# Products in turn, later joins and a third pair of seven products in a two-layer encoder kernel

## The chip, the core and the metric

The kernel runs as one program on one core of a Trainium2 chip. The metric is the device time of one execution in microseconds (us). TensorE does the matrix products, VectorE (DVE in the profile) and ScalarE (ACT) do the elementwise work, SyncE (SP) issues nearly all transfers, and GpSimd (POOL) does a few small operations.

## The reference: what is computed

Two layers run over a sequence of 256 tokens with a model width of 2048, all in float32. In each layer:

- `h = RMSNorm(x)`, then one input projection gives queries, keys, values and two gating inputs (width 3584 in all);
- eight heads of windowed attention, with two key/value heads, rotary embedding, norms of queries and keys, and a learned sink in the softmax;
- a spatial gating part: GELU, a LayerNorm, a 128x128 product per head along the sequence, and a multiplication;
- both results are normalised, joined and projected back by `w_o`, and the residual is added;
- a feed-forward part: `x + W_down(silu(g) * u)`, where `[g | u]` is a three-tap depthwise convolution over the sequence of `RMSNorm(x) @ w_up`, with a hidden width of 5632.

## The kernel before, in words

**Three products for one.** The products must be as good as float32, and TensorE takes them in a shorter type. So every operand is split into a high part and a low part. For activations and weights `(a_hi + a_lo)(w_hi + w_lo)` the kernel computes `a_hi w_hi`, `a_lo w_hi` (these two are called high products here, since they use the high part of the weights) and `a_hi w_lo` (the low product). Each weight piece is loaded into a `raw` tile, ScalarE copies it to `hi` (line 154), and VectorE subtracts to get `lo` (line 142). There are four `raw` buffers, three `hi` and three `lo`.

**Blocks.** The usual block is 1 MB of weights: four slices of 128 rows by 512 columns. `rows_by_cols` (line 175; its matmul is line 181) runs 24 matmuls on it: 16 high products over all four slices, then the 8 low products. The input projection, `w_o` and `w_up` use it; `direct` (its matmul is line 209) does the same for `w_down`. In the input projection and the first half of `w_o` a block is split in two pieces of 1024 columns (`step`), and the first two blocks of the program in four. `unit` (lines 325 and 330) handles the gate input the other way round, with the weights stationary: 32 high products of 512 columns, then 32 low products of 256.

**Seven products.** In the down projection some pairs of slices for a pair of column groups are done by a scheme with seven products in place of eight (`seven`, lines 239 to 287). It needs sums of weight slices (lines 249 to 251), splits two tiles (lines 245 and 252 on ScalarE, two subtractions of line 142 on VectorE), so it takes two `hi` and two `lo` buffers, and runs 21 matmuls (lines 269, 270 and 275) where 24 would stand. The mixes of the activations that it needs are made by `mixed` when these activations are finished. `seven_out` adds its four sums into the residual.

**The feed-forward part** runs in two halves of the hidden width (`HALVES`): 20 slices, then 24. In each half, `gate_and_up` makes four slices at a time: g rows and u rows by 4 blocks each, then `leave` takes them out of PSUM (lines 914 and 916 on ScalarE) and asks for transposes by DMA; when these have landed, ScalarE puts the words together (`together`, line 495), and the convolution, the activation and the multiplication follow on both engines. Then the down projection of that half runs in two groups, each for a pair of column groups. `FAST` says which pairs of slices go by seven: two pairs in both groups of the first half, four pairs in the first group of the second half.

**The order of the work.** Steps that are to follow later are put in a list, `waiting`; `let_in` runs everything in it, and is called inside each block after its second slice. `after(n, step)` makes a step wait for n more such calls. The queue of each engine is put in order at build time by the framework's scheduler: of the instructions that it takes to be ready it chooses the one with the highest priority, with its own estimates for when things are ready. Priority follows the program's order, with the parts under `urgent()` first. `issue_after` ties only instructions of TensorE to their place. On the chip, each queue runs strictly in the order that the scheduler made.

Of the kernel before, what the change touches and what calls it, by code (L numbers as in the profile page):

```python
# [25 lines left out]
NK = D // P  # L26
NF = DFF // P
W = 512
KB = 4
# [4 lines left out]


HALVES = ((0, 20), (20, NF))
FAST = ((4, 10), (4, 8, 12, 16))
AFTER = (2, 4, 5, 6)


# [26 lines left out]
def encoder(ctx: ExitStack, tc: tile.TileContext, xT, x, w_in, w_gu, w_o, w_up, w_down, wsT, pcol, prow, rope, out):  # L67
# [97 lines left out]
    def after(n, step):  # L165
        waiting.append(step if n == 0 else lambda: after(n - 1, step))

    def let_in():
        for step in waiting[:]:
            waiting.remove(step)  # L170
            with tc.issue_after(latest()), urgent():
                step()


    def rows_by_cols(ps, acts, src, first, last, raw=None, apart=False, step=4 * W):

        hi, lo = split_weights(src, raw, step)

        def product(m, kk, part):
            w = (hi if part < 2 else lo)[:, kk * W : (kk + 1) * W]  # L180
            nc.tensor.matmul(  # L181
                ps[m], acts[kk][:, part % 2, m * P : (m + 1) * P], w,
                start=first and kk == 0 and part == 0, stop=last and kk == KB - 1 and part == 2,
            )

        if apart:
            for m in range(2):
                for kk in range(KB):
                    for part in range(3):
                        product(m, kk, part)  # L190
            return
        for kk in range(KB):
            for m in range(2):
                product(m, kk, 0)
                product(m, kk, 1)
            if kk == 1:
                let_in()
        for kk in range(KB):
            for m in range(2):
                product(m, kk, 2)  # L200
# [38 lines left out]
    def seven(left, right, more, acts, mix, src, used_left, used_right, first, last):  # L239
        with urgent():  # L240
            raw = raw_tile()
            nc.sync.dma_start(raw, src)
            sums = raw_tile()
            hi, lo, his, los = hi_tile(), lo_tile(), hi_tile(), lo_tile()
            nc.scalar.activation(hi[:, : 3 * W], raw[:, : 3 * W], AF.Copy)
            b = raw.rearrange("p (g c) -> p g c", c=W)
            s = sums.rearrange("p (g c) -> p g c", c=W)
            b12 = b[:, 3:4, :].to_broadcast([P, 2, W])
            nc.vector.tensor_tensor(out=s[:, 0:2, :], in0=b12, in1=b[:, 0:3:2, :], op=ALU.add)
            nc.vector.tensor_tensor(out=s[:, 2, :], in0=s[:, 0, :], in1=b[:, 2, :], op=ALU.add)  # L250
            nc.vector.tensor_tensor(out=s[:, 3, :], in0=s[:, 2, :], in1=b[:, 1, :], op=ALU.add)
            nc.scalar.activation(his, sums, AF.Copy)  # L252
            lo_part(lo[:, : 3 * W], raw[:, : 3 * W], hi[:, : 3 * W])
            lo_part(los, sums, his)

        def own(kk, m):
            return [acts[kk][:, j, m * P : (m + 1) * P] for j in range(2)]

        def mix_of(j):
            return [t[:, j * P : (j + 1) * P] for t in mix]  # L260

        used_more = set() if first else set(range(4))
        low = []

        def product(ps, used, m, a, w, g):
            cs = slice(g * W, (g + 1) * W)
            new = m not in used
            used.add(m)
            nc.tensor.matmul(ps[m], a[0], w[0][:, cs], start=new, stop=False)  # L269
            nc.tensor.matmul(ps[m], a[1], w[0][:, cs], start=False, stop=False)  # L270
            low.append((ps, m, a, w, cs))

        def lows():
            for ps, m, a, w, cs in low:
                nc.tensor.matmul(ps[m], a[0], w[1][:, cs], start=False, stop=ps is more and last)  # L275
            low.clear()

        product(left, used_left, 0, own(1, 0), (hi, lo), 1)
        product(right, used_right, 0, mix_of(3), (hi, lo), 2)
        product(more, used_more, 0, own(0, 0), (hi, lo), 0)  # L280
        lows()
        product(more, used_more, 1, mix_of(2), (his, los), 2)
        product(more, used_more, 2, mix_of(1), (his, los), 0)
        product(more, used_more, 3, mix_of(0), (his, los), 1)
        product(left, used_left, 1, own(1, 1), (his, los), 3)
        lows()
# [17 lines left out]
    def take(steps):  # L304
        for step in steps:
            with tc.issue_after(latest()):
                step()


    def unit(acts, w, steps=()):  # L310
        ps = mm()
        his, los = [], []
        for b in range(0, NK, UB):
            h, lo = split_weights(w[:, b * UW : (b + UB) * UW], None, 2 * W)
            his.append(h)
            los.append(lo)

        def tile_of(tiles, k, i):
            c = k % UB * UW + i * P
            return tiles[k // UB][:, c : c + P]  # L320

        for k in range(NK):
            for i in range(2):
                x1 = acts[k].rearrange("p a b -> p (a b)")
                nc.tensor.matmul(ps[:, i, :], tile_of(his, k, i), x1, start=k == 0, stop=False)  # L325
            if k == 5:
                let_in()
        for k in range(NK):
            for i in range(2):
                nc.tensor.matmul(  # L330
                    ps[:, i, :SEQ], tile_of(los, k, i), acts[k][:, 0, :], start=False, stop=k == NK - 1
                )
            if k == 0:
                take(steps)
        return ps


# [344 lines left out]
    NB = NK // KB  # L682
    for l in range(DEPTH):
        pc, qk = params
        acts = hT

        def in_rows(ps, c, b):
            src = w_in[l, c, :, b * KB * W : (b + 1) * KB * W]
            raw = first_raws.pop(0) if l == 0 and first_raws else None
            step = 2 * W if raw is None else W  # L690
            rows_by_cols(ps, acts[b * KB : b * KB + KB], src, b == 0, b == NB - 1, raw, step=step)


        psk, psq = mm(), mm()
# [27 lines left out]
        atts = []  # L722
# [41 lines left out]
        first = group_steps(0, psq)  # L764
        first()
        ps = chunk(1, [[sent_keys], [turned_keys, first], [], [first]] if l else [[], [], [sent_keys, first], [turned_keys]])
# [8 lines left out]
        for i in range(2):  # L775
# [4 lines left out]
            ps = chunk(3 + i, between[i])  # L780
# [73 lines left out]
        gates = []  # L854
# [6 lines left out]
        def out_rows(half, c, r):  # L861
            t = mm()
            ps = [t[:, m, :] for m in range(2)]
            for b in range(2):
                src = w_o[l, c, :, (half * 2 + b) * KB * W : (half * 2 + b + 1) * KB * W]
                rows_by_cols(ps, (atts, gates)[half][b * KB : b * KB + KB], src, b == 0, b == 1, step=4 * W if half else 2 * W)
            residual(ps, c, r)

        ra = inv_rms_cols(acca, D // 2, "a")
# [36 lines left out]
            src = w_up[l, n * (NF // 4) + j, :, b * KB * W : (b + 1) * KB * W]  # L906
            rows_by_cols([ps[:, m, :] for m in range(2)], acts2[b * KB : b * KB + KB], src, b == 0, b == NB - 1)

        def leave(ps, then):
            halves = []  # L910
            for m in range(2):
                rows = ev().rearrange("p a b -> p (a b)")
                with urgent():
                    nc.scalar.activation(rows, ps[:, m, :], AF.Copy, scale=r2[:, m : m + 1])  # L914
                h = sl([P, 2, 2, SEQ], U16)
                nc.scalar.copy(h, rows.bitcast(U16).rearrange("p (j n b) -> p j b n", j=2, b=2))  # L916
                halves.append(h)
            tall = [sl([P, 4, SEQ], U16) for _ in range(2)]

            def asked():  # L920
                for j in range(2):
                    for m in range(2):
                        half = halves[m][:, j, :, :].rearrange("p b n -> p (b n)")
                        nc.sync.dma_start_transpose(tall[j][:, :, m * P : (m + 1) * P], half)
                after(2, lambda: then(tall))

            waiting.append(asked)

        def gate_and_up(j, ys, mixes):
# [22 lines left out]
            if j == 0:  # L952
                pss = [mm(), mm()]
                for b in range(NB):
                    for n in range(2):
                        up_rows(pss[n], n, j, b)
                        if b == NB - 1:
                            leave(pss[n], (gate_in, up_in)[n])
                return
            for n in range(2):  # L960
                ps = mm()
                for b in range(NB):
                    up_rows(ps, n, j, b)
                leave(ps, (gate_in, up_in)[n])

        w_at = 0
        for half, (f0, f1) in enumerate(HALVES):
# [5 lines left out]
            last = f1 == NF  # L973
# [19 lines left out]
            for group in range(2):  # L993
# [4 lines left out]
                for n, (cs, ks, sevenfold) in enumerate(blocks):  # L998
# [6 lines left out]
                    src = w_down[l, :, w_at : w_at + len(cs) * len(ks) * W]  # L1005
                    w_at += len(cs) * len(ks) * W
                    acts = [ys[k - f0] for k in ks]
# [88 lines left out]
```

## Time and profile before

| | |
|---|---|
| Median of 3 runs | 1971.12 us (1969.78 to 1973.15) |
| Time of the profiled execution | 1969.81 us |
| Its span, first to last instruction | 1968.0 us |
| TensorE busy with matmuls | 1954.8 us, 8832 matmuls |
| VectorE busy | 1334.6 us |
| ScalarE busy | 1318.1 us |
| Data moved | 414.02 MB, 210 GB/s on average |
| Granted TensorE clock | 1.000 |

The time of an execution is 1.8 us longer than its span; the span runs from the first to the last instruction. Matmuls overlap in the records: one of 512 columns is recorded with 389 ns, but the next one starts earlier, so the distance between starts is what counts. In a group of instructions the last columns are busy time, mean duration of one, and idle time of the engine just before these instructions with what ended it. In the waits, each line gives the total, the number of times, and the longest.

### The profile page before, as it was taken

To read this page: it belongs to the slowest core of one execution; us is meant where nothing else is said; L and a number is where in the kernel's file an instruction comes from. 1 tells how busy PE (TensorE), PEld (TensorE's weight loads), DVE (VectorE), ACT (ScalarE), POOL (GpSimd) and SP (SyncE) were. 2 spreads that over 40 slices of the span, in tenths; PEclk is the share of its full clock that TensorE was granted. 3 is DMA by queue.
4 is the path that set the end of the run, shared out by engine and by line. 5 is a ranking of instruction groups with operands and counts; after the bars stand their busy time and mean duration, and the time that the engine had idled before them with its cause. 6 is when DMAs were issued, how large, how long until landed. Compare 5 with 4: busy or idle time off the path is not lost.

```text
span 1968.0 us, 22935 instructions
## 1 busy us (share of the span) xinstructions
PE 1954.8 (99%) x8832; PEld 1622.1 (82%) x8832; DVE 1334.6 (68%) x1628; ACT 1318.1 (67%) x1437; POOL 22.9 (1%) x25
## 2 busy tenths in 40 slices
PE   9999999999999999999999999999999999999999
PEld 7878888888788888888888888888888888888887
DVE  6768775666874666688566696756668655666873
ACT  6667487687644777776666774877885456777742
POOL 0000000000000000000000000000000000000000
PEclk9999999999999999999999999999999999999999
DMA  9763486776665677757767546867766667677572
GB/s 373 218 213 141 171 235 190 220 227 195 217 235 187 217 226 223 213 174 246 231 205 221 172 150 203 242 199 222 217 197 218 214 205 223 214 217 224 169 267 86
DMA packets 190733, 414.02 MB, mean 210 GB/s; under 512 B 139424, under 2 KB 140704, under 8 KB 145568
## 3 DMA queue, kind: packets, MB, share of 16 engines
q1 hardware_dynamic: 189904, 411.83, 66.1%
q8 instruction: 69, 1.13, 0.2%
q10 hardware_dynamic: 720, 0.73, 0.1%
q14 instruction: 40, 0.33, 0.1%
HBM read 378.43 MB, written 2.10 MB: 193 GB/s over the span
## 4 chain that ended last, share of the span: by engine, by line
PE 87%; ACT 5%; DMA 3%; DVE 3%; issue 2%; SPq 0%; DVEq 0%; ACTq 0%
PE mm L181 59%; PE mm L209 17%; DMA sl<-sl 3%; PE mm L325 3%; ACT hi L154 2%; PE tp L209 2%; DVE lo L142 2%; PE mm L330 1%; ACT sl L916 1%; PE mm L275 1%; PE mm L270 1%; PE mm L269 1%; ACT sl L914 1%; ACT sl L495 1%; DVE sl L897 0%
## 5 line engine op out<-in xcount | busy, mean ns | idle before, releaser
L142 DVE TENSOR_TENSOR lo<-raw,hi 128x2048 fp32r<-128x2048 f32 (+3 forms) x444 | 839.0, 1904 | 491.0 <-ACT hi L154 442.2
L181 PE MATMUL mm<-hi,sl 128*128 128x512 f32 x3968 | 943.4, 389 | 0.9 <-ACT hi L154 0.8
L154 ACT ACTIVATE hi<-raw 128x2048 fp32r<-128x2048 f32 (+2 forms) x412 | 650.3, 1594 | 364.8 <-PE mm L181 171.7
L181 PEld LDWEIGHTS mm<-hi,sl 128*128 128x128 f32 x3968 | 744.4, 188 | 156.1 <-ACT hi L154 1.7
L181 PE MATMUL mm<-lo,sl 128*128 128x512 f32 x1984 | 491.3, 389 | 0.0
L181 PEld LDWEIGHTS mm<-lo,sl 128*128 128x128 f32 x1984 | 372.1, 188 | 76.9
L209 PE MATMUL mm<-hi,sl 128*128 128x512 f32 x1056 | 250.4, 389 | 1.9 <-ACT hi L154 1.9
L209 PEld LDWEIGHTS mm<-hi,sl 128*128 128x128 f32 x1056 | 198.1, 188 | 43.8 <-ACT hi L154 2.8
L495 ACT COPY sl<-sl 128x1024 uint16<-128x1024 uint16 x98 | 132.5, 1352 | 134.7 <-DMA sl<-sl 134.5
L209 PE MATMUL mm<-lo,sl 128*128 128x512 f32 x528 | 130.4, 389 | 0.0
L209 PEld LDWEIGHTS mm<-lo,sl 128*128 128x128 f32 x528 | 99.1, 188 | 20.5
L896 ACT ACTIVATE sl<-sl,pc 128x256 f32<-128x256 f32 x176 | 95.8, 590 | 1.3
L916 ACT COPY sl<-sl 128x1024 uint16<-128x1024 uint16 x88 | 92.0, 1046 | 2.6
L897 DVE SCALAR_TENSOR_TENSOR sl<-sl,pc 128x255 f32<-128x255 f32 x176 | 77.9, 478 | 8.1 <-ACT sl L896 8.0
L900 DVE SCALAR_TENSOR_TENSOR sl<-sl,pc 128x255 f32<-128x255 f32 x176 | 77.9, 478 | 0.7
L325 PE MATMUL mm<-sl,hi 128*128 128x512 f32 x256 | 63.7, 394 | 1.6 <-ACT sl L784 1.6
L356 ACT ACTIVATE sl<-sl 128x256 fp32r<-128x256 f32 x88 | 31.7, 408 | 46.7 <-DVE sl L944 46.7
L914 ACT ACTIVATE sl<-mm,yr 128x512 f32<-128x512 f32 x88 | 59.7, 678 | 0.0
L325 PEld LDWEIGHTS mm<-sl,hi 128*128 128x128 f32 x256 | 46.8, 188 | 10.6 <-ACT sl L784 1.8
L349 DVE SCALAR_TENSOR_TENSOR sl<-sl,pc 128x256 fp32r<-128x256 f32 x96 | 42.1, 479 | 17.6 <-ACT sl L348 17.4
L348 ACT ACTIVATE sl<-sl,pc 128x256 fp32r<-128x256 f32 x96 | 43.0, 498 | 2.3 <-DMA sl<-in_xT 1.1
L252 ACT ACTIVATE hi<-raw 128x2048 fp32r<-128x2048 f32 x16 | 30.6, 1914 | 19.2 <-PE mm L209 14.1
(144 smaller groups left out, 1062.5 us busy)
## 6 DMA issues: line engine op xcount, KB each, us to landing
raw<-in_w_up SPq DMA_DIRECT2D x176, 1024.0 KB, 5.0
raw<-in_w_down SPq DMA_DIRECT2D x88, 1024.0 KB, 4.8
raw<-in_w_in SPq DMA_DIRECT2D x38, 1024.0 KB, 5.1
raw<-in_w_o SPq DMA_DIRECT2D x32, 1024.0 KB, 5.0
raw<-in_w_gu SPq DMA_DIRECT2D x16, 1024.0 KB, 5.4
sl<-sl SPq DMA_TRANSPOSE x244, 4.3
sl<-in_prow SPq DMA_DIRECT2D x12, 256.0 KB, 7.4
raw<-in_w_in SPq DMA_DIRECT2D x8, 256.0 KB, 5.3
```

What stands on the lines that cost most here:

```text
L142: nc.vector.tensor_tensor(out=lo, in0=part, in1=hi.bitcast(F32), op=ALU.subtract)
L154: nc.scalar.activation(hi[:, cs], raw[:, cs], AF.Copy)
L181: nc.tensor.matmul(ps[m], acts[kk][:, part % 2, m * P : (m + 1) * P], w, start=first and kk == 0 and part == 0, stop=last and kk == KB - 1 ...
L209: nc.tensor.matmul(ps[m], acts[kk][:, part % 2, m * P : (m + 1) * P], w, start=first, stop=done and kk == len(acts) - 1 and part == 2,)
L325: nc.tensor.matmul(ps[:, i, :], tile_of(his, k, i), x1, start=k == 0, stop=False)
L348: nc.scalar.activation(t[:, 0, :], src, AF.Copy, scale=g)
L495: nc.scalar.copy(words, tall.rearrange("p (b a) n -> p b (a n)", b=2))
L896: nc.scalar.activation(t[:, i, :], s[:, i, :], AF.Identity, bias=col(3), scale=col(1))
L897: nc.vector.scalar_tensor_tensor(out=t[:, i, 1:], in0=s[:, i, : SEQ - 1], scalar=col(0), in1=t[:, i, 1:], op0=ALU.mult, op1=ALU.add)
L900: nc.vector.scalar_tensor_tensor(out=t[:, i, : SEQ - 1], in0=s[:, i, 1:], scalar=col(2), in1=t[:, i, : SEQ - 1], op0=ALU.mult, op1=ALU.add)
L914: nc.scalar.activation(rows, ps[:, m, :], AF.Copy, scale=r2[:, m : m + 1])
L916: nc.scalar.copy(h, rows.bitcast(U16).rearrange("p (j n b) -> p j b n", j=2, b=2))
```

## The change

There are five edits.

1. `FAST` for the first half becomes (4, 8, 12) in place of (4, 10): three pairs of slices by seven products instead of two. The four column pairs concerned are two in each of the two layers. The 14 slices that are left are no multiple of 4, so the last plain block of each column group has two slices.
2. `rows_by_cols` gets `in_turn`: for each slice the four high products are followed at once by its two low products. The input projection (all blocks through `in_rows`) and the first half of `w_o` use it. The unused branch `apart` of this function goes.
3. `seven` calls `let_in` once, after its first low products.
4. `unit` runs its low products with the column half outside and the slice inside, and takes the `steps` after the second low product of the first half.
5. `leave` gets the number of calls to wait before the transposes are put together: 3 for the last group of four slices in each half, 2 as before for the others. The first group (`j == 0`) keeps 2.

```diff
-FAST = ((4, 10), (4, 8, 12, 16))
+FAST = ((4, 8, 12), (4, 8, 12, 16))
...
-    def rows_by_cols(ps, acts, src, first, last, raw=None, apart=False, step=4 * W):
+    def rows_by_cols(ps, acts, src, first, last, raw=None, in_turn=False, step=4 * W):
...
-        if apart:
-            for m in range(2):
-                for kk in range(KB):
-                    for part in range(3):
-                        product(m, kk, part)
-            return
         for kk in range(KB):
             for m in range(2):
                 product(m, kk, 0)
                 product(m, kk, 1)
+            if in_turn:
+                for m in range(2):
+                    product(m, kk, 2)
             if kk == 1:
                 let_in()
+        if in_turn:
+            return
         for kk in range(KB):
             for m in range(2):
                 product(m, kk, 2)
...
         product(more, used_more, 0, own(0, 0), (hi, lo), 0)
         lows()
+        let_in()
         product(more, used_more, 1, mix_of(2), (his, los), 2)
...
-        for k in range(NK):
-            for i in range(2):
+        for i in range(2):
+            for k in range(NK):
                 nc.tensor.matmul(
                     ps[:, i, :SEQ], tile_of(los, k, i), acts[k][:, 0, :], start=False, stop=k == NK - 1
                 )
-            if k == 0:
-                take(steps)
+                if i == 0 and k == 1:
+                    take(steps)
...
-            rows_by_cols(ps, acts[b * KB : b * KB + KB], src, b == 0, b == NB - 1, raw, step=step)
+            rows_by_cols(ps, acts[b * KB : b * KB + KB], src, b == 0, b == NB - 1, raw, True, step)
...
-                rows_by_cols(ps, (atts, gates)[half][b * KB : b * KB + KB], src, b == 0, b == 1, step=4 * W if half else 2 * W)
+                rows_by_cols(ps, (atts, gates)[half][b * KB : b * KB + KB], src, b == 0, b == 1, None, half == 0, 4 * W if half else 2 * W)
...
-        def leave(ps, then):
+        def leave(ps, then, wait):
...
-                after(2, lambda: then(tall))
+                after(wait, lambda: then(tall))
...
-                            leave(pss[n], (gate_in, up_in)[n])
+                            leave(pss[n], (gate_in, up_in)[n], 2)
...
-                leave(ps, (gate_in, up_in)[n])
+                leave(ps, (gate_in, up_in)[n], 2 + (j == f1 // 4 - 1))
```

## The prediction, made before the changed kernel was built or run

> **What bounds the kernel now.** I read the page's totals first, then the chain that ended last, then what TensorE waited for.
>
> ```profile
> span 1968.0 us, 22935 instructions
> PE 1954.8 (99%) x8832; PEld 1622.1 (82%) x8832; DVE 1334.6 (68%) x1628; ACT 1318.1 (67%) x1437; POOL 22.9 (1%) x25
> PE 87%; ACT 5%; DMA 3%; DVE 3%; issue 2%; SPq 0%; DVEq 0%; ACTq 0%
> ...
> 599.80 261.12 PE mm L181 x1152
> ...
> PE tp L369 <- DVE sl L363: 3.2, 1, 3.2
> PE mm L209 <- ACT hi L154: 1.9, 2, 1.4
> PE mm L325 <- ACT sl L784: 1.6, 1, 1.6
> ...
> PE mm L181 <- ACT hi L154: 0.8, 1, 0.8
> PE tp L368 <- DVE sl L363: 0.7, 1, 0.7
> PE tp L368 <- ACT sl L362: 0.2, 1, 0.2
> ```
>
> TensorE is the bound from end to end. The fifth line is a piece of the chain in the second half's up projection of the first layer: 1152 matmuls of 512 columns in 261.12 us, so 226.67 ns from start to start, with nothing between. The waits add up to under 9 us, so there are only two ways to win much: fewer matmuls, or those few waits. Everything else in the change can only cost, unless it moves one of the six waits shown.
>
> **Edit 1, the third pair.** It is in two column pairs of each of two layers, so four more blocks of 21 matmuls stand where 24 stood: 12 matmuls, 12 x 226.67 ns = **2.72 us less**.
>
> [...]
>
> What the scheme costs lies on the other engines:
>
> ```profile
> L142 DVE TENSOR_TENSOR lo<-raw,hi 128x2048 fp32r<-128x2048 f32 x280 | 640.7, 2289 | 419.4 <-ACT hi L154 387.7 <-ACT hi L252 28.9 <-PE mm L181 2.3
> L142 DVE TENSOR_TENSOR lo<-raw,hi 128x1536 fp32r<-128x1536 f32 x16 | 28.0, 1752 | 0.4 <-PE mm L181 0.4
> L249 DVE TENSOR_TENSOR raw<-raw 128x1024 f32<-128x1024 f32 x16 | 19.5, 1221 | 3.7 <-DMA raw<-in_w_down 3.5
> L250 DVE TENSOR_TENSOR raw<-raw 128x512 f32<-128x512 f32 x16 | 11.1, 691 | 0.5
> L251 DVE TENSOR_TENSOR raw<-raw 128x512 f32<-128x512 f32 x16 | 11.0, 688 | 0.3
> ...
> core 0: us, PE busy (x) PEld busy (x) DVE busy (x) ACT busy (x) POOL busy (x), PEclk, DMA share, GB/s
> 470.00:525.00 55.00, 53.63 (x237) 44.11 (x236) 43.83 (x50) 43.38 (x46) 0.00 (x0) 1.00 0.63 195
> 855.00:918.00 63.00, 63.00 (x280) 52.18 (x279) 51.58 (x48) 42.44 (x37) 0.00 (x0) 1.00 0.65 223
> ```
>
> On VectorE a block by seven takes 1.22 + 0.69 + 0.69 + 1.75 + 2.29 = 6.64 us where a plain one takes 2.29, so 4.35 us more per pair, against 21 x 0.2267 = 4.76 us of matmuls; ScalarE has room. The cover is VectorE's idle time. In the last row, the second half's first column pair, four such blocks follow each other with one plain block between, exactly the density that the first half gets. VectorE is busy 51.58 of 63 us there, and TensorE 63.00 of 63.00. Around the first half's start it is busy 43.83 of 55; with 4.35 more it would be 48.2 of about 54, or 89%, denser than the row that is shown to work, because the last convolutions fall in here. So I cost it at nothing, with bounds from 0 to 4 x 4.35 = 17.4 us, should no idle time serve. Each pair also gets one more transfer, and each layer one more mix of activations; these lie in the same idle time.
>
> **Edits 5 and 3, the joins.** The wait of line 209 (1.9 us in two places) is this, in the first layer's first half:
>
> ```profile
> 475.57 3.79 PE L181 MATMUL mm<-hi,sl 128*128 128x512 f32 x16
> ...
> 479.56 1.91 ACT L154 ACTIVATE hi<-raw 128x2048 fp32r<-128x2048 f32 x1
> 484.07 1.37 ACT L495 COPY sl<-sl 128x1024 uint16<-128x1024 uint16 x1 [2.60 <-DMA sl<-sl]
> 485.30 1.90 ACT L154 ACTIVATE hi<-raw 128x2048 fp32r<-128x2048 f32 x1
> ...
> 498.02 1.91 ACT L252 ACTIVATE hi<-raw 128x2048 fp32r<-128x2048 f32 x1
> 505.20 1.36 ACT L495 COPY sl<-sl 128x1024 uint16<-128x1024 uint16 x1 [5.27 <-DMA sl<-sl]
> 506.60 0.60 ACT L896 ACTIVATE sl<-sl,pc 128x256 f32<-128x256 f32 x1
> 507.11 1.90 ACT L154 ACTIVATE hi<-raw 128x2048 fp32r<-128x2048 f32 x1
> ...
> 509.06 3.25 PE L209 MATMUL mm<-hi,sl 128*128 128x512 f32 x13 [1.37 <-ACT hi L154]
> ```
>
> ScalarE stands at the head of its queue before a join (line 495) whose transposes have not landed, first for 2.60 us and then for 5.27 us; behind it the copy to `hi` for the next block ends at 509.01, and TensorE starts at 509.06. With a wait of 3, the g rows' join is written one block later, behind the copy at 485.30. That copy can then run in the 2.60 us of idle time (of the three buffers, the one that it takes was last read by the matmuls of the row at 475.57, which end by 479.4), and all that follows on ScalarE moves up by about 1.9 us, including the copies that the second transposes wait for. That takes the 1.4 us away, and the 0.5 us of the other layer: **1.9 us less**. The u rows' join does not move: it now waits for one call more, and the `let_in` in `seven` is that call more; it does nothing else, and costs nothing. Bounds: 1.9 us less, or nothing, if the scheduler puts the joins where they were.
>
> **Edit 2, products in turn.** No matmul is added. The low part of a block's first piece is needed 4 matmuls after the block's start instead of 16 (2.7 us earlier), and `hi` is given back after 22 instead of 16 (1.36 us later). Is there cover?
>
> ```profile
> L181 PE MATMUL mm<-lo,sl 128*128 128x512 f32 x1984 | 491.3, 389 | 0.0
> L154 ACT ACTIVATE hi<-raw 128x1024 fp32r<-128x1024 f32 x140 | 141.3, 1050 | 108.0 <-PE mm L181 63.1 <-issue 18.1 <-PE mm L325 10.6
> ```
>
> The low products never waited. Most of ScalarE's idle time before these copies ended when TensorE gave a buffer back: it runs ahead by all three buffers, two blocks or about 10.9 us, so the splits are early by more than both shifts together. Cost nothing, except at the start:
>
> ```profile
> 4.78 0.69 DVE L142 TENSOR_TENSOR lo<-raw,hi 128x512 fp32r<-128x512 f32 x1 [0.60 <-ACT hi L154]
> 5.34 2.48 PE L181 MATMUL mm<-hi,sl 128*128 128x512 f32 x8
> 6.58 0.69 DVE L142 TENSOR_TENSOR lo<-raw,hi 128x512 fp32r<-128x512 f32 x1 [0.72 <-ACT hi L154]
> 8.65 2.42 PE L181 MATMUL mm<-hi,sl 128*128 128x512 f32 x8 [0.83 <-ACT hi L154]
> 10.92 2.01 PE L181 MATMUL mm<-lo,sl 128*128 128x512 f32 x8
> ...
> 26.20 0.17 DVE L462 TENSOR_SCALAR nsink<-qk 128x8 f32<-128x8 f32 x1 [4.06 <-DMA qk<-in_prow]
> 32.78 0.87 DVE L349 SCALAR_TENSOR_TENSOR sl<-sl,pc 128x256 fp32r<-128x256 f32 x2
> ```
>
> Here TensorE waits for the third slice until 8.65 while the low parts of the first two are ready by 7.27. In turn, four or six low products fill that hole and the next, and the block ends 4 x 0.23 to 6 x 0.23 = 0.9 to 1.4 us earlier. But VectorE stands until 26.20 for a transfer, and delivers the third activations of a later block only at 33.3, whatever TensorE does. How much is kept depends on which products the scheduler puts before that point: all of it, or a stricter order that leaves TensorE idle there, 1.2 us of loss (two blocks in turn have 24 products left at 33.3 if two half blocks were let in before, 36 if one was, so 12 x 0.23 = 2.7 us between the two cases). I take the middle, **0.7 us less**; bounds 1.4 less to 1.2 more.
>
> **Edit 4, the units.** The same 32 low products. The first `lo` tile is now free after 24 of them instead of 16:
>
> ```profile
> 127.24 3.83 PE mm L330 x32
> ...
> 142.44 4.63 DVE L142 TENSOR_TENSOR lo<-raw,hi 128x1024 fp32r<-128x1024 f32 x4 [1.64 <-PE mm L330]
> 146.99 0.68 DVE L363 TENSOR_TENSOR sl<-tp,sl 128x512 fp32r<-128x512 f32 x1
> 147.72 0.50 PE L369 MATMUL tp<-sl 128*128 128x512 f32 x1 [3.16 <-DVE sl L363]
> ```
>
> 8 x 3.83/32 = 0.96 us later. This is where the largest wait arises: VectorE waits for a `lo` buffer, then makes four pieces, and only then the split on which TensorE already waits. If the order of the queues stayed, the wait would grow by up to 0.96 us. But the order is made anew, since so many products have moved; the waits of attention (3.2 + 1.6 + 0.7 + 0.2 = 5.7 us) are an accident of the present order. Bounds: 5.7 us less to 8 units x 0.96 = 7.7 us more. I take 0.
>
> **Sum.** 2.72 + 1.9 + 0.7 = 5.3 us less. The profiled execution has a span of 1968.0 us and took 1969.81 in all, so 1964.5; it lies 1.31 us under the median of the runs shown, so on the median's scale **1965.8 us**.
>
> **Rivals.**
>
> A. *The joins stay.* The scheduler takes what it holds to be ready; the row at 505.20 shows a join ahead of a copy that stands earlier in the program. If that also holds for the g rows, the 1.9 us stay: 1971.1 - 2.7 - 0.7 = 1967.7. Against it: at 484.07 the join stands just where the program has it.
>
> B. *The waits of attention go too*, in the new order: 5.3 + 5.7 = 11.0 less, 1960.1. For it: the second layer runs nearly the same steps, and of the waits listed 0.9 us are its own against 4.8 of the first's. Against: nothing in the change aims at the split of line 363.
>
> C. *The held `lo` tile blocks VectorE in every unit*: 7.7 us more than forecast, 1973.5. For it: the row at 142.44. Against: in the second layer the same queue waits far less.
>
> D. *VectorE becomes the bound in the first halves*: with the lead used up, each added block's 4.35 us shows at TensorE. This is the case on the other side: at full price 1965.8 + 17.4 = 1983.2, and slower than before once 1.3 us per pair are exposed (5.3 / 4). For it: at 509.06 the lead is already nil. Against: the row of the second half.
>
> **How the numbers follow.** Forecast 0.43, A 0.20, B 0.20, C 0.10, D 0.07. A measurement of this kernel can tell about 0.2% from no change, 3.9 us: faster is under 1967.2, slower over 1975.1. Forecast: 0.33 under, 0.10 within (the start or a part of the joins lost). A: 0.07 and 0.13. B: 0.20 under. C: 0.02, 0.06, and 0.02 over. D: 0.02 within, 0.05 over. In all faster 0.62, same 0.31, slower 0.07. The range of the forecast alone is 1963 to 1968.5; to hold 8 in 10 it reaches to B, with 3 us of the start's and edit 4's bounds, and to C: 1957 to 1974. What lies outside is most of D and the ends of B and C.
>
> **What would show it.** Step 1: 8820 matmuls, 20 blocks by seven instead of 16, and no wait of TensorE for `lo` or `hi` inside the first halves' down projections; such waits would mean D. Joins: no wait of line 209 behind the first block by seven, and a copy to `hi` ahead of the g rows' join; the same 1.4 and 0.5 us would mean A. In turn: low products of the first block before 8.65 us, and the place of the tenth block about 0.7 us earlier. Attention: waits of lines 363, 368, 369 and 784 near 5.7 us in all; near 0 is B, over 10 is C. The forecast is wrong if the matmuls' pace is not 226.7 ns, or if a new wait of over 3 us appears where the trace of before has none.

## The result, and the profile after

The changed kernel takes **1975.21 us** (median of 20 executions, 1973.86 to 1976.89) against 1971.97 us of the kernel before, timed beside it (1968.59 to 1974.56). The ratio is 1.0017, with a 95% interval from 1.0010 to 1.0024. So it is a little slower, by 3.2 us, and not 5.3 us faster, and it lies above the range of the prediction. The profiled execution took 1975.69 us, with a span of 1973.9 us, 5.9 us more than before; the spans differ by more than the medians because the profiled execution of the kernel before lies 2.2 us under the median given here. The granted clock was 0.997 in place of 1.000.

The totals of the page after:

```profile
span 1973.9 us, 22972 instructions
PE 1955.6 (99%) x8820; PEld 1622.6 (82%) x8820; DVE 1351.8 (68%) x1656; ACT 1323.1 (67%) x1447; POOL 20.4 (1%) x25
```

There are 8820 matmuls, 12 fewer, as forecast. VectorE has 17.2 us more to do, close to the 4 x 4.35 = 17.4 us of the four added blocks by seven. TensorE's recorded busy time grew although it has fewer matmuls, so some of them were slower.

What TensorE waited for (total, times, longest, in us):

```profile
PE tp L368 <- DVE nmx L558: 5.4, 1, 5.4
PE tp L368 <- DVE sl L363: 5.1, 1, 5.1
PE mm L325 <- ACT sl L784: 1.4, 1, 1.4
```

The wait of the down projection for `hi` (1.9 us at line 209 before; that matmul is now line 208) is gone. In attention there are now two waits of over 5 us, both of line 368, the first of the three matmuls that make one product of attention (`matmul3`, lines 368 to 370; their result goes to a PSUM tile `tp`). Before, the largest was 3.2 us. Both lie where VectorE makes `lo` parts, as the timeline after shows (start, duration, engine, and at the end the idle time before with its releaser):

```profile
5.24 1.17 PE L181 MATMUL mm<-hi,sl 128*128 128x512 f32 x4
6.26 0.62 PE L181 MATMUL mm<-lo,sl 128*128 128x512 f32 x2
...
142.21 4.63 DVE L142 TENSOR_TENSOR lo<-raw,hi 128x1024 fp32r<-128x1024 f32 x4 [1.60 <-PE mm L330]
...
146.76 0.68 DVE L363 TENSOR_TENSOR sl<-sl 128x512 fp32r<-128x512 f32 x1
147.36 1.28 DVE L363 TENSOR_TENSOR sl<-tp,sl 128x512 fp32r<-128x512 f32 x2
...
148.19 0.77 PE L368 MATMUL tp<-sl 128*128 128x512 f32 x1 [5.06 <-DVE sl L363]
...
148.75 0.63 PE L369 MATMUL tp<-sl 128*128 128x512 f32 x1
149.18 0.63 PE L370 MATMUL tp<-sl 128*128 128x512 f32 x1
...
486.04 3.71 ACT L154 ACTIVATE hi<-raw 128x2048 fp32r<-128x2048 f32 x2
...
498.25 1.34 ACT L495 COPY sl<-sl 128x1024 uint16<-128x1024 uint16 x1
...
1130.00 4.63 DVE L142 TENSOR_TENSOR lo<-raw,hi 128x1024 fp32r<-128x1024 f32 x4
...
1135.34 0.47 DVE L558 CUSTOM_DVE_ANT_0 sl<-tp,mask,qs 128x256 f32<-128x256 f32 x1
...
1136.28 0.58 PE L368 MATMUL tp<-sl 128*128 128x256 f32 x1 [5.37 <-DVE nmx L558]
```

In the first layer the four `lo` pieces (142.21 to 146.84) now have three splits of line 363 behind them, one at 146.76 and two from 147.36. Before, a single one stood behind them (row 146.99 of the prediction). TensorE, at a product of the values with the softmax's weights, goes on only when the second of the three is done, so it stands for 5.06 us. In the second layer four `lo` pieces, which waited for nothing, stand ahead of line 558, which takes scores out of PSUM and so frees the buffer that the products of queries and keys at 1136.28 write. The kernel before had the same instructions in another order there:

```profile
1125.89 0.47 DVE L558 CUSTOM_DVE_ANT_0 sl<-tp,mask,qs 128x256 f32<-128x256 f32 x1
...
1129.65 1.22 DVE L142 TENSOR_TENSOR lo<-raw,hi 128x1024 fp32r<-128x1024 f32 x1
...
1131.40 1.21 DVE L142 TENSOR_TENSOR lo<-raw,hi 128x1024 fp32r<-128x1024 f32 x1
```

There the scores left first, and the `lo` pieces came behind them, one or two at a time, with no wait of TensorE.

A second loss follows each of the two waits. In the windows of the kernel after, PEclk (behind the five engines) is the granted clock:

```profile
core 0: us, PE busy (x) PEld busy (x) DVE busy (x) ACT busy (x) POOL busy (x), PEclk, DMA share, GB/s
146.00:149.00 3.00, 0.81 (x2) 0.75 (x3) 2.64 (x4) 0.00 (x0) 0.00 (x0) 0.50 0.90 358
149.00:152.00 3.00, 3.00 (x11) 2.54 (x11) 0.00 (x0) 0.84 (x2) 0.00 (x0) 0.51 0.76 306
...
1136.30:1139.60 3.30, 3.30 (x14) 3.20 (x15) 2.69 (x13) 2.33 (x8) 0.00 (x0) 0.50 0.84 350
1139.60:1143.00 3.40, 3.40 (x12) 2.71 (x11) 3.33 (x14) 2.75 (x6) 0.00 (x0) 0.68 0.00 0
...
470.00:525.00 55.00, 55.00 (x244) 45.56 (x243) 46.56 (x56) 43.40 (x45) 0.00 (x0) 1.00 0.55 179
525.00:600.00 75.00, 75.00 (x333) 62.10 (x332) 64.24 (x57) 36.48 (x25) 0.00 (x0) 1.00 0.63 230
```

Around the waits the clock is granted at 0.50. Matmuls of 512 columns behind the first wait start 0.43 us apart (148.75, 149.18, 149.61) where the pace is 0.227. The last two rows are the first half's start and its down projection: TensorE is busy in all of both.

Where the 5.9 us of the span went, by the distances from one matmul's start to the next, less the median of these distances in the traces (227, 120 and 111 ns for 512, 256 and 128 columns):

| stretch | after minus before, us |
|---|---|
| 12 matmuls fewer | -2.7 |
| start, 0 to 40 us | -0.5 |
| around the waits of line 209 (500 to 520, 1480 to 1500) | -2.6 |
| attention of the first layer, 100 to 240 us (7.3 became 10.7) | +3.3 |
| attention of the second layer, 1040 to 1220 us (2.7 became 11.0) | +8.3 |
| sum | +5.8 |

Of the 11.6 us lost in attention, the two waits themselves make 1.9 (5.1 for 3.2) and 5.4. By the same distances, the slow matmuls behind them lost 1.8 us behind the first and 2.6 us behind the second. Together that is 11.7 us; the rest, a few tenths in each layer, lies in short waits.

### The profile page after: what moved, and what is told of

It reads as the page before. It is cut to its first block, busy times and chain, and to the rows that moved or that the text cites. A ratio compares the mean times of both kernels' runs of the same rounds, so it can differ in the third digit from the quotient of the medians.

```text
span 1973.9 us, 22972 instructions
## 1 busy us (share of the span) xinstructions
PE 1955.6 (99%) x8820; PEld 1622.6 (82%) x8820; DVE 1351.8 (68%) x1656; ACT 1323.1 (67%) x1447; POOL 20.4 (1%) x25
## 4 chain that ended last, share of the span: by engine, by line
PE 96%; DMA 1%; DVE 1%; ACT 1%; issue 0%; SPq 0%; DVEq 0%; ACTq 0%
PE mm L181 66%; PE mm L208 17%; PE mm L325 3%; PE tp L208 2%; PE mm L330 1%; PE mm L268 1%; PE mm L274 1%; PE mm L269 1%; DVE lo L142 1%; DMA raw<-in_w_in 1%; PE tp L368 0%; DMA qk<-in_prow 0%; PE tp L269 0%; PE tp L274 0%; PE tp L268 0%; PE tp L370 0%
## 5 line engine op out<-in xcount | busy, mean ns | idle before, releaser
L181 PEld LDWEIGHTS mm<-hi,sl 128*128 128x128 f32 x3968 | 743.4, 188 | 156.1 <-DVE sl L349 1.4
L154 ACT ACTIVATE hi<-raw 128x2048 fp32r<-128x2048 f32 (+2 forms) x412 | 643.6, 1577 | 332.1 <-PE mm L181 172.7
L181 PE MATMUL mm<-lo,sl 128*128 128x512 f32 x1984 | 517.6, 389 | 0.0
L181 PEld LDWEIGHTS mm<-lo,sl 128*128 128x128 f32 x1984 | 372.3, 188 | 77.4 <-DVE lo L142 0.2
L208 PEld LDWEIGHTS mm<-hi,sl 128*128 128x128 f32 x992 | 186.2, 188 | 38.6
L208 PE MATMUL mm<-lo,sl 128*128 128x512 f32 x496 | 123.1, 389 | 0.0
L208 PEld LDWEIGHTS mm<-lo,sl 128*128 128x128 f32 x496 | 93.1, 188 | 19.3
L251 ACT ACTIVATE hi<-raw 128x2048 fp32r<-128x2048 f32 x20 | 38.3, 1914 | 27.7 <-DVE raw L250 25.7
L244 ACT ACTIVATE hi<-raw 128x1536 fp32r<-128x1536 f32 x20 | 29.8, 1488 | 23.6 <-PE mm L181 13.9
```

The lines of the kernel that those rows point to most:

```text
L154: nc.scalar.activation(hi[:, cs], raw[:, cs], AF.Copy)
L181: nc.tensor.matmul(ps[m], acts[kk][:, part % 2, m * P : (m + 1) * P], w, start=first and kk == 0 and part == 0, stop=last and kk == KB - 1 ...
L208: nc.tensor.matmul(ps[m], acts[kk][:, part % 2, m * P : (m + 1) * P], w, start=first, stop=done and kk == len(acts) - 1 and part == 2,)
```

## The experiments

Each ratio below is against the kernel before, run on the same chip, with its 95% interval. The question after the profile was which of the edits makes the two waits in attention, and by what: by the order in which VectorE's queue was put together, or by the longer hold of a `lo` tile (the prediction's rival C). The expectations are told as they stood when each was written.

**The change without edit 4.**

```diff
-        for i in range(2):
-            for k in range(NK):
+        for k in range(NK):
+            for i in range(2):
...
-                if i == 0 and k == 1:
-                    take(steps)
+            if k == 0:
+                take(steps)
```

> The change without edit 4: the units' low products run with the slice outside again, the rest of the change stays. Theory 1 (edit 4 gives both lo tiles of a unit back at its end, so that VectorE stands and then makes four pieces while TensorE waits): the waits of 5.4 and 5.1 us before line 368 go, what stays is about the 5.7 us of before, and the time is 8 to 10 us under the changed kernel's 1975.2, about 1966. Theory 2 (the products in turn have moved the order of attention, edit 2 alone is the cause): the two waits stay, time within 1.5 us of 1975. Theory 3 (any new order of the queues can have such waits, neither edit is the cause by itself): anything between, with waits at other places.

Measured: 1973.56 us, ratio 1.0007 (0.9998 to 1.0017). The waits of TensorE:

```profile
PE tp L368 <- DVE nmx L558: 5.0, 1, 5.0
PE tp L368 <- DVE sl L363: 4.1, 1, 4.1
```

Both waits are there without edit 4. The first layer's is 4.1 us instead of 5.1, the size of the 0.96 us by which edit 4 holds the first `lo` tile. The timelines agree: the four `lo` pieces start 3.07 us after the low products begin in the changed kernel (139.14 to 142.21) and 2.11 us after them here (139.43 to 141.54), again 0.96 us apart. So the prediction's rival C had the mechanism for about 1 us of one wait, and something else makes the waits.

**The change without edit 2.**

```diff
-            rows_by_cols(ps, acts[b * KB : b * KB + KB], src, b == 0, b == NB - 1, raw, True, step)
+            rows_by_cols(ps, acts[b * KB : b * KB + KB], src, b == 0, b == NB - 1, raw, step=step)
...
-                rows_by_cols(ps, (atts, gates)[half][b * KB : b * KB + KB], src, b == 0, b == 1, None, half == 0, 4 * W if half else 2 * W)
+                rows_by_cols(ps, (atts, gates)[half][b * KB : b * KB + KB], src, b == 0, b == 1, step=4 * W if half else 2 * W)
```

> The change without edit 2: high products of a block first, then its low products, everywhere; edits 1, 3, 4 and 5 stay. Theory 1 (edit 4 is the cause): the two waits of over 5 us before line 368 stay, time within 1.5 us of 1975, or 0.6 us over it, since the start loses what products in turn gave it. Theory 2 (edit 2 is the cause): the two waits go, about 1966. Theory 3: waits elsewhere.

Measured: 1971.38 us, ratio 0.9993 (0.9982 to 1.0004). Its waits (the lines are one further down in this kernel):

```profile
PE tp L370 <- DVE sl L364: 3.6, 1, 3.6
PE tp L813 <- issue: 2.3, 1, 2.3
PE tp L369 <- ACT sl L363: 1.7, 2, 1.5
```

The 5.4 us wait for line 558 is gone, but other waits stand in attention. Each of the two edits disturbs the order there in its own way.

**Edits 1, 3 and 5 alone.** Both edits above are undone.

```diff
-FAST = ((4, 10), (4, 8, 12, 16))
+FAST = ((4, 8, 12), (4, 8, 12, 16))
...
         lows()
+        let_in()
...
-                leave(ps, (gate_in, up_in)[n])
+                leave(ps, (gate_in, up_in)[n], 2 + (j == f1 // 4 - 1))
```

> The third pair, the let_in in it and the later joins alone (edits 1, 3 and 5; 2 and 4 undone). By the terms of the prediction: 2.7 us for 12 matmuls and 1.9 to 2.4 us for the waits of line 209, so 4.6 to 5.1 us under before, a ratio of 0.9974 to 0.9977; attention as before with its 5.7 us of waits. By the rival that the third pair makes VectorE the bound: not faster than before, with waits of TensorE for lo or hi in the first halves' down projections. By theory 3 attention could also be ordered anew here, though nothing of it is edited.

Measured: 1965.34 us, ratio 0.9963 (0.9949 to 0.9977). Attention is as before (one wait of 3.2 us, VectorE's instructions in the same order), and no wait of the down projection is left. Its span is 5.1 us under that of the kernel before and its median 6.1 us; the forecast for these edits was 2.72 + 1.9 = 4.6 us. From here, by the medians on the same chip, edit 2 costs 1973.56 - 1965.34 = 8.2 us, edit 4 costs 6.0 us. The two costs don't add up: the changed kernel, which has both, lies 9.9 us above this one.

**Edit 4 alone**, on the kernel before.

```diff
-        for k in range(NK):
-            for i in range(2):
+        for i in range(2):
+            for k in range(NK):
...
-            if k == 0:
-                take(steps)
+                if i == 0 and k == 1:
+                    take(steps)
```

> The kernel before with edit 4 alone. Theory 1: the two long waits are here too, with the half clock behind them; 6 to 9 us over before, a ratio of 1.003 to 1.0045. Theory 2: no wait over 3.5 us, a ratio of 0.999 to 1.001. Theory 3: either.

Measured: 1975.67 us, ratio 1.0018 (1.0009 to 1.0028). Two of its waits are those of the kernel without edit 2 (3.6 us for line 363, and 2.3 us of line 812, a matmul of the spatial gating), and line 209 waits 2.6 us. So edit 4 alone makes the kernel slower by about 3.5 us, where I had put 0.

**Edit 2 alone**, on the kernel before.

```diff
             for m in range(2):
                 product(m, kk, 0)
                 product(m, kk, 1)
+            if in_turn:
+                for m in range(2):
+                    product(m, kk, 2)
...
+        if in_turn:
+            return
```

> Products in turn alone (edit 2). Predicted term: 0.7 us less at the start, nothing in attention, a ratio of 0.9997. By what the runs have shown since, that VectorE's queue of attention is put in another order when the blocks before it change: two waits of 4 to 5 us before line 368, with half clock behind them, as in the changed kernel without edit 4; 6 to 8 us over before, a ratio of 1.003 to 1.004.

Measured: 1979.1 us, ratio 1.0037 (1.0025 to 1.0050).

```profile
PE tp L367 <- DVE nmx L557: 5.0, 1, 5.0
PE tp L367 <- DVE sl L362: 4.1, 1, 4.1
PE mm L208 <- ACT hi L154: 2.6, 2, 1.5
```

These are the waits of the change without edit 4 (one line further up here), and the joins' wait with them. Edit 2 does the larger part of the harm, though none of its own blocks waits for a `lo` part.

**Edit 1 alone**, on the kernel before.

```diff
-FAST = ((4, 10), (4, 8, 12, 16))
+FAST = ((4, 8, 12), (4, 8, 12, 16))
```

> The third pair alone, without the later joins and without the let_in in it. Predicted term: 12 matmuls, 2.7 us less than before, a ratio of 0.9986; TensorE's two waits of line 209 (1.9 us in all) stay as they were. If the third pair used up VectorE's lead, more waits of this line or of 269, and a ratio of 0.999 or over. If it alone removed the waits of line 209, a ratio of 0.9975.

Measured: 1968.24 us, ratio 0.9975 (0.9966 to 0.9984), so 0.25% or 4.9 us less (3.8 us by the medians). No wait of the down projection for `hi` is left in this profile either, although the joins wait for two calls as before. So the third pair brings its matmuls, and it takes the joins' wait away by itself.

**Edits 3 and 5 alone**, on the kernel before.

```diff
         lows()
+        let_in()
...
-                leave(ps, (gate_in, up_in)[n])
+                leave(ps, (gate_in, up_in)[n], 2 + (j == f1 // 4 - 1))
```

> The later joins alone (edits 3 and 5; the blocks by seven stay at two pairs). Predicted term: TensorE's two waits of line 209, 1.9 us, go; a ratio of 0.9988 to 0.9992. By rival A (the scheduler leaves the joins where they were): the waits of 1.4 and 0.5 us stay, a ratio of 0.9995 to 1.0005.

Measured: 1970.54 us, ratio 0.9994 (0.9985 to 1.0003). The wait of line 209 is gone here too, but what that brings can't be told from no change.

**Attention's steps first.** If the order of VectorE's queue is the cause, then putting the steps of attention ahead of the `lo` pieces in that queue must take the waits away. Three kernels get the same edit: the changed one, the one with edits 1, 3 and 5, and the one before.

```diff
     def take(steps):
         for step in steps:
-            with tc.issue_after(latest()):
+            with tc.issue_after(latest()), urgent():
                 step()
```

On the changed kernel:

> The changed kernel with the attention steps of `take` under urgent. Theory (TensorE waits since attention's splits stand behind four low-part pieces that wait for a lo buffer): the waits of 5.4 and 5.1 us before line 368 and both stretches of half clock go, and the time falls by 9 to 14 us from 1975.2, to 1961 to 1966, although edits 2 and 4 are still in. Rival (edits 2 and 4 cost by themselves, since lo is held longer, whatever stands in the queue): not under 1971.

Measured: **1957.88 us** (1957.79 to 1959.9), ratio 0.9930 (0.9918 to 0.9943), 17.3 us less than the changed kernel (by the ratios, 0.9930 against 1.0017, it is the same). Its span is 1956.1 us, and its waits are:

```profile
PE tp L120 <- DVE ones L116: 1.1, 1, 1.1
PE tp L368 <- DVE sl L363: 0.7, 2, 0.4
```

The same place of the first layer in its timeline:

```profile
138.85 0.69 DVE L363 TENSOR_TENSOR sl<-tp,sl 128x512 fp32r<-128x512 f32 x1 [0.66 <-ACT sl L362]
...
140.28 0.69 DVE L363 TENSOR_TENSOR sl<-tp,sl 128x512 fp32r<-128x512 f32 x1 [0.74 <-ACT sl L362]
...
144.69 1.23 DVE L142 TENSOR_TENSOR lo<-raw,hi 128x1024 fp32r<-128x1024 f32 x1
```

The splits come first, the `lo` pieces behind them and one at a time, and both waits are gone; the clock is 1.000. That settles the cause: the waits came from the order in which the queues were put together, not from what edits 2 and 4 ask of TensorE, which are both still in. The edit gives these steps priority on every engine; that VectorE's queue is the one that counts is read from the rows above. This version beats both kernels.

On edits 1, 3 and 5:

> Edits 1, 3 and 5 alone, and the attention steps that `take` puts into the units and blocks get the priority of the weight splits (take under urgent as well). In the trace of edits 1, 3 and 5 alone TensorE still waits 3.2 us for one split of line 364 that stands behind four low-part pieces in VectorE's queue, with 3.4 us of half clock behind it. Theory: it is this place in the queue that costs. Then the wait goes and the clock stays at 1.0, and the time falls by 4 to 7 us from 1965.3, to about 1960. Rival (attention is bound by the work of VectorE, not by its order): other waits of the same sum, 1964 to 1967. Second rival: the blocks' low parts come late instead, with waits of line 181 or 325, over 1967.

Measured: 1958.86 us, ratio 0.9934 (0.9921 to 0.9946). With attention's steps first, edits 2 and 4 bring nothing that can be measured (0.9930 against 0.9934).

On the kernel before:

> The kernel before with one edit that the change doesn't have: the attention steps of `take` under urgent. If the place in VectorE's queue is what made the waits of attention in the kernel before as well (3.2 and 1.6 us, and the clock behind them), it gains 5 to 9 us, a ratio of 0.9955 to 0.9975, and what the five edits are worth with attention out of the way is the distance from here to the changed kernel with the same edit (ratio 0.993): 4 to 9 us. If it gains nothing, the gain there came from the five edits.

Measured: 1965.42 us, ratio 0.9969 (0.9956 to 0.9981). Line 209 still waits, 2.1 us in two places. The span is 1963.7 us, so the five edits are worth 1963.7 - 1956.1 = 7.6 us (the ratios, 0.9969 and 0.9930, say the same) where attention doesn't depend on the accident of the order; the forecast for them was 5.3.

**A fourth `lo` buffer** in the changed kernel, its room taken from the slots.

```diff
-    slots = pool("slots", 54)
+    slots = pool("slots", 50)
...
-    lop = pool("lop", 3)
+    lop = pool("lop", 4)
```

> The changed kernel with four lo buffers in place of three; to make room the shared slots go from 54 to 50. Theory: VectorE makes the units' low parts before TensorE has given the earlier ones back, so they no longer stand between TensorE and the split; the two waits go, 1961 to 1967. If the shared slots were the scarcer thing, there are new waits, in the feed-forward part too, and the time is over 1975. Rival (lo is not what VectorE waits for): the two waits stay, about 1975.

Measured: 1970.3 us, ratio 0.9990 (0.9981 to 0.9998).

```profile
PE tp L368 <- DVE sl L363: 3.5, 2, 2.8
PE tp L368 <- DVE nmx L558: 2.3, 1, 2.3
```

The two waits shrink from 5.1 and 5.4 us to 2.8 and 2.3, and don't go, and new ones come (1.6 us of line 181 for line 349, 1.1 us of line 369). So a shortage of `lo` buffers is at most a part of the waits. How large a part can't be told: with another buffer and fewer slots the order is made anew as well.

**What a pause does to the clock.** In the changed kernel with attention's steps first, ten pauses of TensorE were put into the second half's up projection of the first layer: four transposes, k subtractions of 128x512 on VectorE one behind the other, one transpose of the result, and the matmuls that follow are tied behind it.

```diff
+        PAUSES = (2, 9, 4, 7, 1, 8, 3, 6, 5, 10)
...
+                for i in range(k):
+                    nc.vector.tensor_tensor(out=a, in0=a if i else t, in1=xr[:, 0, :W], op=ALU.subtract)
...
+                    nc.tensor.transpose(t2, a[:, :P], ident)
```

> Measures the price of a pause of TensorE by itself. Base: the changed kernel with the steps under urgent, which has no half clock anywhere. In the second half's up projection of the first layer, ten times, all following matmuls are held behind a chain on VectorE of 1 to 10 subtractions of 128x512 (about 0.69 us each), in mixed order: pauses of about 1.5 to 8 us; nothing is left out of the computation. [...]

Measured, in one execution: 2042.34 us, clock 0.984. The tenth pause, the longest, fell together with matmuls of the down projection, which were not tied, and didn't happen; the other nine did, as the row of the waits shows.

```profile
PE tp L943 <- DVE sl L940: 56.5, 9, 10.2
```

Three of them in the timeline, with the length of the pause in brackets:

```profile
650.14 0.47 PE L943 MATMUL tp<-ident,sl 128*128 128x128 f32 x1 [3.41 <-DVE sl L940]
...
685.62 0.45 PE L943 MATMUL tp<-ident,sl 128*128 128x128 f32 x1 [10.20 <-DVE sl L940]
...
775.19 0.35 PE L943 MATMUL tp<-ident,sl 128*128 128x128 f32 x1 [2.68 <-DVE sl L940]
```

The windows behind these three, with the columns as in the windows above:

```profile
650.10:653.50 3.40, 3.36 (x9) 2.69 (x10) 2.81 (x7) 0.83 (x3) 0.00 (x0) 0.50 0.68 277
653.50:656.90 3.40, 3.40 (x12) 2.66 (x11) 0.38 (x2) 1.18 (x2) 0.00 (x0) 0.65 0.00 0
656.90:660.30 3.40, 3.40 (x16) 2.80 (x15) 1.50 (x1) 2.84 (x3) 0.00 (x0) 1.00 0.01 2
...
685.60:689.00 3.40, 3.38 (x9) 2.72 (x10) 0.75 (x2) 0.63 (x1) 0.00 (x0) 0.50 0.00 0
...
775.20:778.60 3.40, 3.40 (x9) 2.75 (x10) 3.23 (x8) 0.88 (x3) 0.00 (x0) 0.52 0.86 304
```

Behind a pause 9 matmuls stand in 3.4 us at 0.50 (650.10) where 16 stand at 1.00 (656.90). All nine pauses, from 2.68 to 10.20 us, were followed by half clock. By the records of the granted clock, it lasted 3.4 us (behind 2.68 and 4.22), 6.8 us (behind 3.41, 5.21, 6.21 and 8.20) or 10.2 us (behind 7.21, 9.20 and 10.20), part of it during the pause itself. So the length alone does not say what follows.

The half clock doesn't go with the transfers either: in the rows at 0.50 and 0.52 the DMA share is 0.68, 0.00 and 0.86, and the kernel without the pauses, with a clock of 1.000, has none.

A wait of 3.2 us, at line 369 in the kernel before (first two rows) and at line 370 with edits 1, 3 and 5 (last two rows), ended in two ways (columns as above):

```profile
142.72:146.13 3.41, 1.85 (x15) 1.63 (x13) 3.41 (x4) 0.00 (x0) 0.00 (x0) 1.00 0.19 24
146.13:149.55 3.42, 1.82 (x11) 1.57 (x12) 1.54 (x2) 1.03 (x2) 0.00 (x0) 1.00 0.85 345
...
143.35:146.76 3.41, 0.66 (x6) 0.45 (x4) 3.41 (x4) 0.00 (x0) 0.00 (x0) 1.00 0.41 115
146.76:150.18 3.42, 3.01 (x12) 2.82 (x13) 0.42 (x2) 1.72 (x4) 0.00 (x0) 0.50 1.00 412
```

In the kernel before, TensorE is busy for 1.85 and 1.82 us of the two rows, and the clock stays at 1.00. With edits 1, 3 and 5 it is busy for 0.66 us of the first row, and the second is granted 0.50. In the same way a wait of 2.3 us with edit 4 alone (line 812) was followed by half clock (0.77 from 1167 to 1170 us, 0.66 from 1170 to 1173), and one of 2.3 us with four `lo` buffers (line 558) was not: the mean clock of that trace, 0.999, leaves room for one stretch of 3.4 us at 0.50 (an estimate: 0.5 x 3.4 of 1967.8 us is 0.0009), and that one lies behind an earlier wait (0.91 from 146 to 150 us, 0.66 from 150 to 154). What decides between the two is not shown.

## Why the prediction was wrong, step by step

**Edit 1: right.** 8820 matmuls; TensorE without a gap in the first halves (55.00 of 55.00 and 75.00 of 75.00 us). The 2.72 us are there, and VectorE's 17 us more are hidden, so rival D fell. (Between the first two of the four blocks by seven in the second half stand two plain blocks, not one; the same holds in the first half, so the comparison of densities stands.)

**Edits 5 and 3: right in size, not in what brings it.** The wait of line 209 is gone, and the stretch around it is 2.6 us shorter for the 1.9 forecast. The two copies to `hi` at 486.04 now stand ahead of the join at 498.25, which no longer waits for its transposes. Rival A fell. But I had made it hang on the wait of 3 alone, and the third pair takes this wait away just as well.

**Edit 2 at the start: the place right, the size not shown.** The first low products stand at 6.26 in place of 10.92, and the first 40 us are 0.5 us shorter, where I had taken 0.7. But they are just as much shorter in profiles without edit 2 (0.5 to 0.6 us in the change without edit 2, with edits 1, 3 and 5, and with edits 3 and 5), and 1.8 us longer with edit 1 alone, which doesn't touch the start. One profile of each kernel can't tell what edit 2 brings there, so that the 0.5 lies near the 0.7 may be luck.

**Edit 2 elsewhere: this is the step that failed.** "Cost nothing, except at the start" followed from the lead of the `hi` and `lo` copies, which is cover for the blocks in question. I looked at whether TensorE would wait for these copies, and it doesn't. I did not ask where in VectorE's queue the `lo` pieces would be put once the low products are wanted earlier. Edit 2 alone costs 0.37%, 7.3 us, through waits of attention's products.

**Edit 4: the same step, failed a second time.** I saw the place ("VectorE waits for a `lo` buffer, then makes four pieces, and only then the split on which TensorE already waits") and that the order would be made anew, called the waits "an accident of the present order", and took the middle, 0. The bounds, 5.7 less to 7.7 more, are the second mistake: attention lost 11.6 us, because a wait can grow by more than the hold of a `lo` buffer, and because the half clock behind a long wait was in no price. The price of rival C was held to be 0.96 us in each unit; what the runs show is two waits in two layers, of which 1 us is that hold.

**The sum.** With attention's steps first, the five edits make 7.6 us, against the 5.3 forecast. Nearly all of the miss, from 5.3 less to 3.2 more by the medians, is therefore the order in attention. (The waits listed before add up to 9.5 us with the 1.1 us of line 120, not to under 9; nothing hangs on it.) Rival B, without the waits of attention, was put at 1960.1 us; the version with attention's steps first, which needs an edit that the change doesn't have, takes 1957.88. "A new wait of over 3 us" was named as what would make the forecast wrong, and that is what came.

## What to carry to other kernels

When a change moves work that a scheduler puts in order at build time, price the new order, not only the work: look at which queue carries both early copies and the steps that TensorE is about to need, and give the latter priority before judging the change. An edit that costs nothing in its own blocks can lose its gain in a part of the kernel that it doesn't touch, and one that seems a loss may only have shuffled that order. A long wait of TensorE is to be priced with slow matmuls behind it: here 1.8 and 2.6 us more for the two waits of over 5 us, and half clock behind each of the nine pauses from 2.68 to 10.20 us.

## What was not expected of the hardware

The half clock was the surprise. It cost the two waits of over 5 us some 1.8 and 2.6 us on top, and the length of a wait alone does not tell whether it comes: a wait of 2.3 us (edit 4 alone) was followed by it, and one of 3.2 us (the kernel before) was not.

The kernel before, with one wait of 3.2 us, spreads over 6.0 us (1968.59 to 1974.56), and the version without any wait over 1.1 us over 2.1 us (1957.79 to 1959.9). The granted clocks fit: of the 29 executions of the kernel before that were timed beside the change without edit 4, the seven at 0.997 took 1974.8 us on average and the ten at 0.999 took 1969.8, and all five of the version without long waits had 1.000. Where the executions of one kernel begin to differ isn't shown, since only one of each left a trace.
